# Weight sums in DRAM tied to the heads of the attention, weight pages of half a unit, row sums made later: a two-layer decoder trunk on one core

## The chip, the cores and the metric

The kernel runs on one core of a Trainium2 chip. The metric is device time in microseconds, from the first to the last instruction of one execution, given as the median of the runs shown. Engines are named as in the profile: PE (TensorE matmul), PEld (its weight load), DVE (VectorE), ACT (ScalarE), POOL (GpSimd) and SP (SyncE, which here only issues transfers). SPq and POOLq are the issuing sides of SP and POOL.

## The reference

Two layers, each ending in x <- LayerNorm(alpha * x + sublayer(x)), for 512 positions of width 2048, all in float32. Cut to what matters here:

```python
def even_layer(x, w_in, conv_w, cmp_pos, cmp_w1, cmp_w2, w_out, rel_table):
    h = x @ w_in
    ...
    y_a = a_b * causal_short_conv(a_c * a_h, conv_w) * jax.nn.silu(a_z)
    y_b = nsa_attention(q, k_c, v_c, k_s, v_s, k_w, v_w, gates, rel_table, cmp_pos, cmp_w1, cmp_w2) * jax.nn.silu(b_z)
    return jnp.concatenate([y_a, y_b], axis=-1) @ w_out

def odd_layer(x, w_in, ln_g, ln_b, sgu_w, sgu_b, w_out):
    h = x @ w_in
    uv = jax.nn.gelu(h[..., :2 * D_SGU])
    z = h[..., 2 * D_SGU:]
    u, v = jnp.split(uv, 2, axis=-1)
    v = layer_norm(v, ln_g, ln_b).reshape(bsz, s // SGU_CHUNK, SGU_CHUNK, SGU_GROUPS, SGU_GROUP_DIM)
    w_causal = sgu_w * jnp.tril(jnp.ones((SGU_CHUNK, SGU_CHUNK), sgu_w.dtype))
    mixed = jnp.einsum('gts,bnsgc->bntgc', w_causal, v) + sgu_b.T[:, :, None]
    y = u * mixed.reshape(bsz, s, D_SGU) * jax.nn.silu(z)
    return y @ w_out
```

The attention has 8 query heads. The layer norm of `v` in the odd layer is folded into the position mixing, and for that the kernel needs the sums over `s` of `w_causal`: the row sums of the position weights.

## The kernel before

**Precision.** Each float32 operand is split into a high and a low part (`split`, L84: ACT writes `hi`, DVE writes `lo` = source minus `hi`), and each product is three matmuls, hi x hi, hi x lo and lo x hi.

**Weights.** A *unit* is 1 MB of weights, 128 partitions by 2048 floats. SP loads it in one transfer into a page `raw` (two pages, L90 and L560), ACT and DVE split it in two halves into pages `whi` and `wlo` (four of each), and PE then runs its matmuls. A page is loaded again only after both of its halves have been split.

**Order of the stages**, as PE runs them:

1. The start: `x` (4 MB) and the first two units come in pieces, and 96 matmuls follow (L138 to L157). Then two units of compressed tokens, the rows of the relative bias (`bias_rows`, L174, and `gcol`, L309, which use `raw` pages as scratch; `rrow` and `rscr` go through DRAM by POOL's queue), two key units with `cmp_half` (L273, weights of the compression, also 1 MB in a `raw` page), and the values of group 0.
2. The heads, h = 0 to 7 (L434). Each has six units of 48 matmuls (query, B gate, and four of the convolution), two score branches, softmax and values. `qT` (L445, one buffer) is the scaled query. The bias tiles `bh` (by SP) and `bc` (by POOL, L439 to L443) have two buffers.
3. The first output product, `strassen(sp, wo0, ...)` (L722), then the product for `v`, `strassen(sp, wv1, ...)` (L763). Each is a Strassen-like product of seven half-size products in the order 1, 2, 5, 3, 6, 7, 4, with four units each and 24 matmuls of 512 columns per unit.
4. The units of `u` and `z` (L808, j = 0 to 15, two units each), with the position mixing (L819).
5. The last product, `strassen(sp, wo1, ...)` (L869), and the last layer norm.

**The weight sums.** The products 5, 7, 6 and 4 take sums of weight blocks. They are made in DRAM by POOL's transfer queue (`weight_sums`, L195): for each sum, a copy of one block into a tile `t[q, g, c]` of 1 MB (L204), then a second transfer that adds the other block to it (L206). There are three sets of 16 sums: `sums0` for `wo0`, `sumsv` for `wv1`, `sums1` for `wo1`. A *step* makes two sums by four transfers of 1 MB. The steps of the first two sets are called two to a head (L458), those of `sums1` after every second j (L825). The copies from the weights read only inputs, and nothing but POOL's own queue, and the sums they build on, holds them back.

**Order on the queues.** The instructions of an engine run in the order of its list; that list is made from the program text, from the tiles' buffers and from what each instruction depends on. An instruction that waits holds all that stand behind it on its engine. SP and POOL each take turns through eight semaphores for their transfers, so a transfer also waits for the one eight before it.

**Row sums.** After the `v` product, L788 multiplies a tile of ones with `swT`, the masked position weights, which DVE makes at L778. PE's next unit (`unit_a`, L101) stands behind it.

Of the kernel before, what the change touches and what calls it, by code (L numbers as in the profile page):

```python
# [16 lines left out]
P = 128  # L17
# [48 lines left out]
def trunk(ctx, tc, xT, xn, oneh, cst, table, wa, wv, convw, posT, cw1, cw2, wo0, wuz, wv1, odg, odb, sguw, sgub, wo1, out):  # L66
# [20 lines left out]

    def load_unit(src, n, cut=1024):

        raw = wp.tile([P, 2048], F32, tag="raw", name="raw", bufs=2)  # L90
        nc.sync.dma_start(raw[:, :n], src)
        parts = []
        for c in range(0, n, cut):
            w = min(cut, n - c)
            hi = wp.tile([P, 1024], F32R, tag="hi", name="whi", bufs=4)
            lo = wp.tile([P, 1024], F32R, tag="lo", name="wlo", bufs=4)
            split(hi[:, :w], lo[:, :w], raw[:, c:c + w])
            parts.append((hi, lo))
        return parts
# [35 lines left out]
    for u in range(2):  # L135
        wraw[u] = wp.tile([P, 2048], F32, tag="raw", name="raw", bufs=2)
    xraw = big.tile([P, KT, S], F32, tag="big0", name="xraw")
    for half in range(2):  # L138
        ws = {}
        for u in range(2):  # L140
            ws[u] = (wp.tile([P, 1024], F32R, tag="hi", name="whi", bufs=4), wp.tile([P, 1024], F32R, tag="lo", name="wlo", bufs=4))
        for i, (k0, k1) in enumerate(XCH[half]):
            for u, w0, w1 in WCH[half][i]:
                nc.sync.dma_start(wraw[u][:, half * 1024 + w0:half * 1024 + w1], wa[u][:, half * 1024 + w0:half * 1024 + w1])
            nc.sync.dma_start(xraw[:, k0:k1, :], xT[:, k0:k1, :])
        for i, (k0, k1) in enumerate(XCH[half]):
            for u, w0, w1 in WCH[half][i]:
                split(ws[u][0][:, w0:w1], ws[u][1][:, w0:w1], wraw[u][:, half * 1024 + w0:half * 1024 + w1])
            split(act_hi[:, k0:k1, :], act_lo[:, k0:k1, :], xraw[:, k0:k1, :])
        for k0, k1 in XCH[half]:  # L150
            for u in range(2):
                hi, lo = ws[u]
                for kt in range(k0, k1):
                    w = slice(kt % 8 * P, kt % 8 * P + P)
                    nc.tensor.matmul(first[u], hi[:, w], act_hi[:, kt, :], start=kt == 0, stop=False)
                    nc.tensor.matmul(first[u], hi[:, w], act_lo[:, kt, :], start=False, stop=False)
                    nc.tensor.matmul(first[u], lo[:, w], act_hi[:, kt, :], start=False, stop=kt == KT - 1)  # L157
# [16 lines left out]
    def bias_rows():  # L174
        half = RLEN // 2
        raw = wp.tile([P, 2048], F32, tag="raw", name="raw", bufs=2)
        oh, tb, rr = raw[:RB + 1, 0:RLEN], raw[:RB + 1, RLEN:RLEN + P], raw[:NH, RLEN + P:2 * RLEN + P]
        nc.sync.dma_start(oh, oneh)
        nc.vector.memset(tb, 0.0)
        nc.vector.memset(tb[:, :NH], NEG)  # L180
        nc.sync.dma_start(tb[:RB, :NH], table)
        for c in range(2):
            ps = bank()
            nc.tensor.matmul(ps[:, :half], tb, oh[:, c * half:(c + 1) * half], start=True, stop=True)
            nc.vector.tensor_copy(rr[:, c * half:(c + 1) * half], ps[:NH, :half])
        nc.gpsimd.dma_start(rrow, rr)
        for h in range(NH):
            nc.gpsimd.dma_start(rscr[h], rrow[h:h + 1].to_broadcast([P, RLEN]))
# [6 lines left out]
    def weight_sums(w, name):  # L195
# [3 lines left out]
        def step(q, gcs):  # L199
            def run():  # L200
                for g, c in gcs:
                    t[q, g, c] = dram.tile([P, 2048], F32, name=f"{name}{q}{g}{c}")
                    first = {5: lambda: blk(w, 0, 0, g, c), 7: lambda: blk(w, 1, 1, g, c), 6: lambda: t[7, g, c], 4: lambda: t[6, g, c]}[q]()
                    nc.gpsimd.dma_start(t[q, g, c], first)  # L204
# [11 lines left out]
    with ExitStack() as es:  # L216
# [56 lines left out]
        def cmp_half(kv, c):  # L273
            if c == 0:
                hps[kv] = bank("hp")
            w1 = wp.tile([P, 16, P], F32, tag="raw", name="raw", bufs=2)
            nc.sync.dma_start(w1, cw1[kv, c])
            for l in range(16):
                nc.tensor.matmul(hps[kv][:, :2 * NCMP], w1[:, l, :], toks[kv][:, c, :, c:c + NCMP, l],
# [29 lines left out]
        gcol = wp.tile([P, 2048], F32, tag="raw", name="raw", bufs=2)[:2 * KT, :P]  # L309
# [124 lines left out]
        for h in range(NH):  # L434
# [23 lines left out]
            for st in (steps0 + stepsv)[2 * h:2 * h + 2]:  # L458
                st()
# [60 lines left out]
    def strassen(sp, w, sums, a, done, given=None, more=2, by_tile=False, wx=None):  # L520
# [37 lines left out]
        def unit(p, g, c):  # L558
            src = sums[p, g, c] if p in (5, 7, 6, 4) else blk(w, *{1: (0, 0), 2: (1, 0), 3: (1, 1)}[p], g, c)
            raw = wp.tile([P, 2048], F32, tag="raw", name="raw", bufs=2)  # L560
            nc.sync.dma_start(raw, src)
            parts = []
            for d in range(2):
                pool = wx if wx and count[0] % 2 else wp
# [3 lines left out]
                split(hi, lo, raw[:, d * 1024:(d + 1) * 1024])  # L568
# [204 lines left out]
    with tc.tile_pool(name="sgu", bufs=2) as sg:  # L773
# [12 lines left out]
        for c in range(2):  # L786
            ps = bank()
            nc.tensor.matmul(ps, ones, swT[:, 4 * c:4 * c + 4, :], start=True, stop=True)  # L788
            nc.vector.tensor_copy(rw[:, 4 * c:4 * c + 4, :], ps.rearrange("p (g t) -> p g t", g=4))
# [18 lines left out]
        for j in range(KT):  # L808
# [7 lines left out]
            nc.vector.scalar_tensor_tensor(th, th, 1.0, ps, ALU.add, ALU.mult)  # L816
            pm = bank("pm")
# [7 lines left out]
            if j % 2 and j < 2 * len(steps1):  # L825
                steps1[j // 2]()
# [129 lines left out]
```

## Time and profile before

| what | value |
| --- | --- |
| median of three runs | 1710.26 us (1708.27 to 1713.61) |
| the profiled execution | 1717.5 us; its span 1715.7 us |
| PE busy | 1629.1 us (95%), 7527 matmuls |
| DVE, ACT, POOL busy | 858.7 us, 584.8 us, 124.8 us |
| mean granted clock of PE | 0.978 |
| moved by the DMA engines | 328.50 MB, of it 217.29 MB by SP's queue and 109.60 MB by POOL's |

The span runs from the first to the last instruction, and the profiled execution's own time has 1.8 us around it. "Busy" counts neither the issuing of transfers nor waiting on semaphores. The granted clock is TensorE's share of its full rate, over the stretch named.

### The profile page before, as it was taken

What the parts mean: (1) busy time and instruction counts of PE and PEld (TensorE: products, weight loads), DVE (VectorE), ACT (ScalarE), POOL (GpSimd) and SP (SyncE); (2) the same over time, 40 slices, a digit from 0 to 9 for tenths busy, and PEclk for the clock granted to TensorE, in tenths of its full rate; (3) what the DMA queues carried; (4) which work ended last, traced back from release to release, by engine and by line L of the source; (5) the groups of instructions that cost most, each with busy time, mean ns of one, the idle gap of its engine ahead of it and who ended that gap; (6) DMA issues with size and microseconds to landing.
All of it is one profiled execution on the core that took longest, in us unless ns stands there. A gap on an engine that the chain in (4) does not pass through costs nothing. (4 is left out here: it accounts for less than half of the span.)

```text
span 1715.7 us, 18770 instructions
## 1 busy us (share of the span) xinstructions
PE 1629.1 (95%) x7527; PEld 1349.5 (79%) x7527; DVE 858.7 (50%) x1323; ACT 584.8 (34%) x859; POOL 124.8 (7%) x188
## 2 busy tenths in 40 slices
PE   5789799999999999999999999997999999999995
PEld 3578688888888888888887778885888888888874
DVE  3211444353524444535655977677533333337678
ACT  3111323232323332323454576541222222226531
POOL 1111111111110000000010000000000000000101
PEclk9889899999999999999999999998999999999998
DMA  9999999999998222222476565576422222218763
GB/s 312 271 291 308 283 295 283 282 294 283 281 269 237 80 99 80 78 95 74 165 218 206 197 221 189 179 282 200 134 99 98 91 81 99 98 58 285 234 187 143
DMA packets 70547, 328.50 MB, mean 191 GB/s; under 512 B 7027, under 2 KB 7827, under 8 KB 46652
## 3 DMA queue, kind: packets, MB, share of 16 engines
q1 hardware_dynamic: 39308, 217.29, 35.5%
q0 software_dynamic: 31008, 109.60, 26.4%
q8 instruction: 59, 0.97, 0.2%
q10 hardware_dynamic: 144, 0.41, 0.1%
q14 instruction: 28, 0.23, 0.0%
HBM read 315.72 MB, written 114.84 MB: 251 GB/s over the span
## 5 line engine op out<-in xcount | busy, mean ns | idle before, releaser
L86 DVE TENSOR_TENSOR wlo<-raw,whi 128x1024 fp32r<-128x1024 f32 (+2 forms) x358 | 427.9, 1206 | 653.1 <-ACT whi L85 647.8
L85 ACT CAST whi<-raw 128x1024 fp32r<-128x1024 f32 (+2 forms) x358 | 366.7, 1037 | 970.9 <-PE ps L109 592.9
L108 PE MATMUL ps<-act_hi,whi 128*128 128x512 f32 x1376 | 545.0, 396 | 10.9 <-ACT whi L85 10.9
L110 PE MATMUL ps<-act_hi,wlo 128*128 128x512 f32 x1376 | 539.3, 392 | 0.8 <-DVE wlo L86 0.7
L109 PE MATMUL ps<-act_lo,whi 128*128 128x512 f32 x1376 | 536.9, 390 | 0.0
L108 PEld LDWEIGHTS ps<-act_hi,whi 128*128 128x128 f32 x1376 | 260.1, 189 | 62.6 <-ACT whi L85 11.0
L110 PEld LDWEIGHTS ps<-act_hi,wlo 128*128 128x128 f32 x1376 | 259.3, 188 | 59.1 <-DVE wlo L86 2.3
L109 PEld LDWEIGHTS ps<-act_lo,whi 128*128 128x128 f32 x1376 | 259.7, 189 | 54.0 <-issue 0.3
L585 PE MATMUL ps<-wlo,shi 128*128 128x512 f32 x576 | 228.1, 397 | 9.6 <-DVE wlo L86 9.5
L584 PE MATMUL ps<-whi,shi 128*128 128x512 f32 x576 | 226.0, 396 | 0.6 <-ACT whi L85 0.6
L586 PE MATMUL ps<-whi,slo 128*128 128x512 f32 x576 | 226.5, 394 | 0.0
L585 PEld LDWEIGHTS ps<-wlo,shi 128*128 128x128 f32 x576 | 109.2, 190 | 38.7 <-DVE wlo L86 15.2
L584 PEld LDWEIGHTS ps<-whi,shi 128*128 128x128 f32 x576 | 109.1, 190 | 24.6 <-ACT whi L85 0.9
L586 PEld LDWEIGHTS ps<-whi,slo 128*128 128x128 f32 x576 | 109.2, 190 | 23.6
L206 POOL DMA_DIRECT2D ts<-in_wo_dram x32 | 33.1, 1033 | 277.2 <-DMA ts<-in_wo_dram 142.9
L625 POOL DMA_DIRECT2D xr<-xres x12 | 10.3, 873 | 458.6 <-DMA raw<-ts 409.4
L371 ACT ACTIVATE t_sc<-t_sc,mx 128x128 f32<-128x128 f32 (+1 forms) x64 | 35.1, 550 | 17.0 <-DVE mx L368 17.0
L117 PE MATMUL ps<-whi,act_hi 128*128 128x268 f32 x128 | 36.9, 288 | 2.2 <-ACT whi L85 2.2
L585 PE MATMUL ps<-wlo,act_hi 128*128 128x512 f32 x96 | 38.5, 401 | 0.2 <-DVE wlo L86 0.2
L584 PE MATMUL ps<-whi,act_hi 128*128 128x512 f32 x96 | 38.6, 404 | 0.0
L586 PE MATMUL ps<-whi,act_lo 128*128 128x512 f32 x96 | 38.2, 398 | 0.0
L118 PE MATMUL ps<-wlo,act_hi 128*128 128x268 f32 x128 | 36.9, 288 | 0.6 <-DVE wlo L86 0.6
(201 smaller groups left out, 1366.9 us busy)
## 6 DMA issues: line engine op xcount, KB each, us to landing
raw<-in_wa_dram SPq DMA_DIRECT2D x54, 1024.0 KB, 8.5
ts<-in_wo_dram POOLq DMA_DIRECT2D x32, 1024.0 KB, 13.7
raw<-ts SPq DMA_DIRECT2D x32, 1024.0 KB, 5.1
raw<-in_wuz_dram SPq DMA_DIRECT2D x32, 1024.0 KB, 4.8
raw<-in_wo_dram SPq DMA_DIRECT2D x24, 1024.0 KB, 4.9
tsv<-in_wv_dram POOLq DMA_DIRECT2D x16, 1024.0 KB, 12.5
raw<-tsv SPq DMA_DIRECT2D x16, 1024.0 KB, 4.8
raw<-in_wv_dram SPq DMA_DIRECT2D x12, 1024.0 KB, 4.8
```

The costliest lines, as they stand in the source:

```text
L85: nc.scalar.copy(hi, src)
L86: nc.vector.tensor_tensor(lo, src, hi.bitcast(F32), ALU.subtract)
L108: nc.tensor.matmul(ps, hi[:, w], act_hi[:, kt, :], start=kt == 0, stop=False)
L109: nc.tensor.matmul(ps, hi[:, w], act_lo[:, kt, :], start=False, stop=False)
L110: nc.tensor.matmul(ps, lo[:, w], act_hi[:, kt, :], start=False, stop=kt == KT - 1)
L117: nc.tensor.matmul(ps[:, :width], act_hi[:, kt, ms], hi[:, w], start=kt == 0, stop=False)
L118: nc.tensor.matmul(ps[:, :width], act_hi[:, kt, ms], lo[:, w], start=False, stop=False)
L206: nc.gpsimd.dma_start(t[q, g, c], blk(w, *{5: (0, 1), 7: (0, 1), 6: (0, 0), 4: (1, 0)}[q], g, c), accum_op=ALU.add, max_dma_last_dim=2048)
L371: nc.scalar.activation(t[:, offs[qb]:offs[qb] + nk], t[:, offs[qb]:offs[qb] + nk], AF.Exp, bias=mx[:, qb:qb + 1], accum_out=sm[:, qb:qb + 1])
L584: nc.tensor.matmul(b, s[0][:, k, ms], hi[:, ws], start=new and c == 0 and k == 0, stop=False, **kw)
L585: nc.tensor.matmul(b, s[0][:, k, ms], lo[:, ws], start=False, stop=False, **kw)
L586: nc.tensor.matmul(b, s[1][:, k, ms], hi[:, ws], start=False, stop=c == 1 and k == 3, **kw)
```

## The change

Three edits.

1. **Ties.** A step takes a small piece of an SBUF tile as an argument. Before each copy it sends four bytes of that piece into the sum's tile in DRAM, and the copy that follows overwrites them. The copy must therefore wait for the four bytes to land, and these for the tile that they are read from. In the attention that tile is `qT` of the head; in the units of `u` and `z` it is `ug` of that j. In turn, the next writer of `qT` or of that `ug` buffer has to wait until the four bytes have been read.
2. **Pages.** `raw` becomes four pages of 1024 floats per partition where it was two of 2048. Each unit is loaded by two transfers of 512 KB (rows of 4 KB per partition, where they were 8 KB), and each page is split and freed alone. Scratch uses of `raw` take one or two of the smaller pages.
3. **Row sums.** The two matmuls with `ones` and the two copies of their results move from ahead of the first unit of stage 4 to behind its second.

```diff
+    def raw_page():
+        return wp.tile([P, 1024], F32, tag="raw", name="raw", bufs=4)
+
     def load_unit(src, n, cut=1024):
-        raw = wp.tile([P, 2048], F32, tag="raw", name="raw", bufs=2)
-        nc.sync.dma_start(raw[:, :n], src)
         parts = []
         for c in range(0, n, cut):
             w = min(cut, n - c)
+            raw = raw_page()
+            nc.sync.dma_start(raw[:, :w], src[:, c:c + w])
             hi = wp.tile([P, 1024], F32R, tag="hi", name="whi", bufs=4)
             lo = wp.tile([P, 1024], F32R, tag="lo", name="wlo", bufs=4)
-            split(hi[:, :w], lo[:, :w], raw[:, c:c + w])
+            split(hi[:, :w], lo[:, :w], raw[:, :w])
...
     def bias_rows():
         half = RLEN // 2
-        raw = wp.tile([P, 2048], F32, tag="raw", name="raw", bufs=2)
-        oh, tb, rr = raw[:RB + 1, 0:RLEN], raw[:RB + 1, RLEN:RLEN + P], raw[:NH, RLEN + P:2 * RLEN + P]
+        raw = raw_page()
+        oh, tb, rr = raw[:RB + 1, 0:RLEN], raw[:RB + 1, RLEN:RLEN + P], raw_page()[:NH, :RLEN]
...
         def step(q, gcs):
-            def run():
+            def run(after=None):
+
                 for g, c in gcs:
                     t[q, g, c] = dram.tile([P, 2048], F32, name=f"{name}{q}{g}{c}")
+                    if after is not None:
+                        nc.gpsimd.dma_start(t[q, g, c][0:1, 0:1], after)
...
-            w1 = wp.tile([P, 16, P], F32, tag="raw", name="raw", bufs=2)
-            nc.sync.dma_start(w1, cw1[kv, c])
+            w1 = [raw_page().rearrange("p (l d) -> p l d", d=P) for _ in range(2)]
+            for i in range(2):
+                nc.sync.dma_start(w1[i], cw1[kv, c][:, 8 * i:8 * i + 8])
...
-        gcol = wp.tile([P, 2048], F32, tag="raw", name="raw", bufs=2)[:2 * KT, :P]
+        gcol = raw_page()[:2 * KT, :P]
...
             for st in (steps0 + stepsv)[2 * h:2 * h + 2]:
-                st()
+                st(qT[0:1, 0:1])
...
-            raw = wp.tile([P, 2048], F32, tag="raw", name="raw", bufs=2)
-            nc.sync.dma_start(raw, src)
             parts = []
             for d in range(2):
+                raw = raw_page()
+                nc.sync.dma_start(raw, src[:, d * 1024:(d + 1) * 1024])
...
-                split(hi, lo, raw[:, d * 1024:(d + 1) * 1024])
+                split(hi, lo, raw)
...
-        for c in range(2):
-            ps = bank()
-            nc.tensor.matmul(ps, ones, swT[:, 4 * c:4 * c + 4, :], start=True, stop=True)
-            nc.vector.tensor_copy(rw[:, 4 * c:4 * c + 4, :], ps.rearrange("p (g t) -> p g t", g=4))
+
+        def row_sums():
+            for c in range(2):
+                ps = bank()
+                nc.tensor.matmul(ps, ones, swT[:, 4 * c:4 * c + 4, :], start=True, stop=True)
+                nc.vector.tensor_copy(rw[:, 4 * c:4 * c + 4, :], ps.rearrange("p (g t) -> p g t", g=4))
...
+            if j == 0:
+                row_sums()
             pm = bank("pm")
...
             if j % 2 and j < 2 * len(steps1):
-                steps1[j // 2]()
+                steps1[j // 2](ug[0:1, 0:1])
```

**What moves on POOL at the start.** In the rows below `bc` is a head's bias tile, `ts0_500` the sum of product 5 for `wo0` with g = 0 and c = 0, and the names in brackets are the semaphores waited for (DMASW and DMAHW are transfers of POOL and SP). Before, POOL's list begins like this:

```order
L439 MEMSET bc_848 128x124
L204 DMA ts0_500_1017<-in_wo0_dram 16x16384
L204 DMA ts0_510_1019<-in_wo0_dram 16x16384
L206 DMA ts0_500_1017<-in_wo0_dram 512x512 [waits DMASW0_49]
L206 DMA ts0_510_1019<-in_wo0_dram 512x512 [waits DMASW1_49]
L204 DMA ts0_501_1023<-in_wo0_dram 16x16384
L204 DMA ts0_511_1025<-in_wo0_dram 16x16384
L206 DMA ts0_501_1023<-in_wo0_dram 512x512 [waits DMASW4_49]
L206 DMA ts0_511_1025<-in_wo0_dram 512x512 [waits DMASW5_49]
L439 MEMSET bc_1447 128x124
```

Of the change, the same engine and place, up to the ties of head 0 (`qT_938`), where `rrow` and `rscr` are the bias rows:

```order
L446 MEMSET bc_1488 128x124
L189 DMA rrow_239<-raw_394 8x640 [waits DVE_49]
L191 DMA rscr_240<-rrow_239 128x640 [waits DMASW0_49]
L191 DMA rscr_240<-rrow_239 128x640 x7
L450 COPY bc_871<-bh_869 128x7 [waits DMAHW1_49,Pool_49]
L450 COPY bc_871<-bh_869 128x15
L450 COPY bc_871<-bh_869 128x23
L450 COPY bc_871<-bh_869 128x31
L450 COPY bc_1488<-bh_1486 128x7 [waits DMAHW2_49,Pool_49]
L450 COPY bc_1488<-bh_1486 128x15
L450 COPY bc_1488<-bh_1486 128x23
L450 COPY bc_1488<-bh_1486 128x31
```

```order
L208 DMA ts0_500_1046<-qT_938 1x1 [waits DMASW1_49,Activation_49]
L208 DMA ts0_510_1049<-qT_938 1x1 [waits DMASW2_49]
L208 DMA ts0_501_1054<-qT_938 1x1 [waits DMASW3_49]
L208 DMA ts0_511_1057<-qT_938 1x1 [waits DMASW4_49]
L210 DMA ts0_500_1046<-in_wo0_dram 16x16384 [waits DMASW5_49,DMASW1_49]
L210 DMA ts0_510_1049<-in_wo0_dram 16x16384 [waits DMASW6_49,DMASW2_49]
L212 DMA ts0_500_1046<-in_wo0_dram 512x512 [waits DMASW7_49,DMASW5_49]
L212 DMA ts0_510_1049<-in_wo0_dram 512x512 [waits DMASW6_49,DMASW0_49]
L210 DMA ts0_501_1054<-in_wo0_dram 16x16384 [waits DMASW3_49]
L210 DMA ts0_511_1057<-in_wo0_dram 16x16384 [waits DMASW4_49]
L212 DMA ts0_501_1054<-in_wo0_dram 512x512 [waits DMASW1_49]
L212 DMA ts0_511_1057<-in_wo0_dram 512x512 [waits DMASW2_49]
```

The first sums have moved from the front of POOL's list to behind the bias rows and the `bc` of two heads, and they wait for ACT's write of `qT`. The later heads follow the same pattern: the `bc` of the head after next, then four ties, then eight transfers.

**What moves on PE between stages 3 and 4.** Before, behind the last matmuls of the `v` product (L584 to L586), with `swT` the masked position weights:

```order
L585 MATMUL ps_7931<-wlo_8143,act_hi_5769 128x512
L586 MATMUL ps_7931<-whi_8142,act_lo_5770 128x512
L788 MATMUL ps_8217<-swT_8205,ones_8210 128x512 [waits DVE_49,PE_49]
L788 MATMUL ps_8220<-swT_8205,ones_8210 128x512
L108 MATMUL ps_8233<-act_hi_5769,whi_8225 128x512 [waits Activation_49]
L109 MATMUL ps_8233<-act_lo_5770,whi_8225 128x512
```

Of the change, the end of the second unit of j = 0, 96 matmuls further on:

```order
L112 MATMUL ps_8567<-act_lo_5933,whi_8563 128x512
L113 MATMUL ps_8567<-act_hi_5932,wlo_8564 128x512
L797 MATMUL ps_8619<-swT_8480,ones_8485 128x512 [waits DVE_49,PE_49]
L797 MATMUL ps_8622<-swT_8480,ones_8485 128x512
L830 MATMUL pm_8625<-swT_8480,xv_5920 128x128 x4
L111 MATMUL ps_8647<-act_hi_5932,whi_8637 128x512 [waits Activation_49]
```

The wait for `swT` now stands behind two units of matmuls.

**What moves on POOL at the end of stage 4.** Of the change: the last step, tied to `ug_10742` of j = 15, stands ahead of the residual additions of `wo1` (L632, which are L625 before), where before all sums of `wo1` stood among the heads:

```order
L208 DMA ts1_401_10818<-ug_10742 1x1 [waits DMASW7_49,DVE_49]
L208 DMA ts1_411_10821<-ug_10742 1x1 [waits DMASW0_49]
L210 DMA ts1_401_10818<-ts1_601_10235 16x16384 [waits DMASW7_49]
L210 DMA ts1_411_10821<-ts1_611_10238 16x16384 [waits DMASW0_49]
L212 DMA ts1_401_10818<-in_wo1_dram 512x512 [waits DMASW1_49]
L212 DMA ts1_411_10821<-in_wo1_dram 512x512 [waits DMASW2_49]
L632 DMA xr_8476<-xres_5938 128x512 [waits DMAHW7_49,DMASW5_49,Activation_49]
```

So the 16 sums of `wo1` have moved from the attention into stage 4, and the last two of them reach into the start of stage 5.

## Rows read from the trace of the kernel before

**Rows 1.** The page: the span, and each engine's busy time.

```profile
span 1715.7 us, 18770 instructions
PE 1629.1 (95%) x7527; PEld 1349.5 (79%) x7527; DVE 858.7 (50%) x1323; ACT 584.8 (34%) x859; POOL 124.8 (7%) x188
```

**Rows 2.** Windows of 50 us: length, busy (count) by engine, clock, DMA share, GB/s.

```profile
0.00:50.00 50.00, 31.39 (x98) 21.32 (x98) 16.90 (x23) 17.55 (x20) 8.40 (x17) 0.93 1.00 312
50.00:100.00 50.00, 37.40 (x149) 28.96 (x147) 11.60 (x17) 4.00 (x4) 7.94 (x12) 0.86 1.04 264
100.00:150.00 50.00, 41.71 (x262) 39.11 (x263) 8.83 (x11) 7.85 (x13) 10.19 (x22) 0.90 1.03 305
150.00:200.00 50.00, 40.98 (x228) 36.31 (x227) 16.50 (x41) 12.63 (x27) 6.17 (x8) 0.90 1.03 295
...
300.00:350.00 50.00, 50.00 (x235) 41.99 (x234) 18.97 (x34) 13.90 (x24) 6.17 (x8) 1.00 1.04 281
...
650.00:700.00 50.00, 50.00 (x239) 42.14 (x238) 18.97 (x35) 14.23 (x24) 0.72 (x4) 1.00 0.27 90
...
1600.00:1650.00 50.00, 50.00 (x219) 40.57 (x217) 28.93 (x27) 27.44 (x32) 6.84 (x8) 1.00 0.79 234
```

**Rows 3.** Waits of PE in the first 210 us: total, times, longest.

```profile
PE ps L108 <- ACT whi L85: 10.9, 1, 10.9
PE ps L155 <- ACT act_hi L85: 10.4, 5, 5.6
PE ps L299 <- DVE rep L297: 9.0, 1, 9.0
PE hp L279 <- DMA raw<-in_cw_dram: 6.4, 1, 6.4
```

**Rows 4.** Timeline of POOL at the start: start, duration, [idle before, releaser].

```profile
1.34 1.24 POOL L204 DMA_DIRECT2D ts<-in_wo_dram  x2
...
98.72 4.15 POOL L188 DMA_DIRECT2D rscr<-rrow  x8 [13.91 <-DMA rrow<-raw]
```

**Rows 5.** Timeline of PE at the start: the first matmul, and two at the slow rate.

```profile
5.55 0.80 PE L155 MATMUL ps<-act_hi,whi 128*128 128x512 f32 x1 [5.55 <-ACT act_hi L85]
...
12.32 0.63 PE L157 MATMUL ps<-act_hi,wlo 128*128 128x512 f32 x1
12.74 0.63 PE L155 MATMUL ps<-act_hi,whi 128*128 128x512 f32 x1
```

**Rows 6.** Windows of 5 us around the row sums, columns as in rows 2.

```profile
1165.00:1170.00 5.00, 0.29 (x1) 0.32 (x2) 4.12 (x7) 0.00 (x0) 1.37 (x1) 0.50 0.80 280
1170.00:1175.00 5.00, 5.00 (x13) 2.86 (x13) 3.17 (x7) 0.00 (x0) 0.00 (x0) 0.73 0.50 170
```

**Rows 7.** All waits of PE: those for the position weights and in the Strassen products.

```profile
PE ps L788 <- DVE swT L778: 10.0, 1, 10.0
PE ps L585 <- DVE wlo L86: 9.7, 9, 3.2
```

**Rows 8.** Timeline of POOL in the attention: the sums of one pair of tiles.

```profile
213.43 1.39 POOL L204 DMA_DIRECT2D tsv<-in_wv_dram  x2
230.93 1.04 POOL L206 DMA_DIRECT2D tsv<-in_wv_dram  x1 [16.11 <-DMA tsv<-in_wv_dram]
...
234.04 0.89 POOL L204 DMA_DIRECT2D tsv<-in_wv_dram  x1
```

**Rows 9.** Timeline of ACT: the `qT` of heads 1 and 2.

```profile
263.03 0.59 ACT L446 ACTIVATE qT<-ps 128x512 f32<-128x512 f32 x1
338.87 0.59 ACT L446 ACTIVATE qT<-ps 128x512 f32<-128x512 f32 x1
```

**Rows 10.** DMA issues: count, KB each, median us from issue to landing.

```profile
raw<-in_wuz_dram SPq DMA_DIRECT2D x32, 1024.0 KB, 4.8
xres<-xr SPq DMA_DIRECT2D x12, 256.0 KB, 2.2
raw<-in_table_dram SPq DMA_DIRECT2D x1, 1.0 KB, 8.4
```

More of the change, by code (lines that the diff above doesn't have):

```diff
@@ L135, in trunk @@
     for u in range(2):
-        wraw[u] = wp.tile([P, 2048], F32, tag="raw", name="raw", bufs=2)
+        wraw[u] = [raw_page(), raw_page()]
     xraw = big.tile([P, KT, S], F32, tag="big0", name="xraw")
@@ L143, in trunk @@
             for u, w0, w1 in WCH[half][i]:
-                nc.sync.dma_start(wraw[u][:, half * 1024 + w0:half * 1024 + w1], wa[u][:, half * 1024 + w0:half * 1024 + w1])
+                nc.sync.dma_start(wraw[u][half][:, w0:w1], wa[u][:, half * 1024 + w0:half * 1024 + w1])
             nc.sync.dma_start(xraw[:, k0:k1, :], xT[:, k0:k1, :])
@@ L147, in trunk @@
             for u, w0, w1 in WCH[half][i]:
-                split(ws[u][0][:, w0:w1], ws[u][1][:, w0:w1], wraw[u][:, half * 1024 + w0:half * 1024 + w1])
+                split(ws[u][0][:, w0:w1], ws[u][1][:, w0:w1], wraw[u][half][:, w0:w1])
             split(act_hi[:, k0:k1, :], act_lo[:, k0:k1, :], xraw[:, k0:k1, :])
@@ L275, in cmp_half @@
                 hps[kv] = bank("hp")
-            w1 = wp.tile([P, 16, P], F32, tag="raw", name="raw", bufs=2)
-            nc.sync.dma_start(w1, cw1[kv, c])
+            w1 = [raw_page().rearrange("p (l d) -> p l d", d=P) for _ in range(2)]
+            for i in range(2):
+                nc.sync.dma_start(w1[i], cw1[kv, c][:, 8 * i:8 * i + 8])
             for l in range(16):
-                nc.tensor.matmul(hps[kv][:, :2 * NCMP], w1[:, l, :], toks[kv][:, c, :, c:c + NCMP, l],
+                nc.tensor.matmul(hps[kv][:, :2 * NCMP], w1[l // 8][:, l % 8, :], toks[kv][:, c, :, c:c + NCMP, l],
                                  start=c == 0 and l == 0, stop=c == 1 and l == 15)
```

## The prediction

> **What bounds the kernel now.** I read the page first: PE is busy for 1629.1 of 1715.7 us, so 86.6 us of idle time and the time that PE works below its full clock are all that this change can give back [rows 1]. Then the windows, to see where they lie. From 200 us on nearly every window is full at clock 1.00, as the one at 300 us; the first four have 31.4, 37.4, 41.7 and 41.0 us busy of 50, at clocks of 0.93, 0.86, 0.90 and 0.90 [rows 2]. So 48.5 us of the idle time lie in the first 200 us. The DMA engines are full there (share 1.00 to 1.04), and the waits of PE name what is missing: weight splits, pieces of `x`, a page of `cw`, and a DVE instruction that stands behind a split [rows 3]. POOL sends its first copies at 1.34 us, before anything needs a sum [rows 4]. At 300 us the DMA engines are as full and PE loses nothing [rows 2]: there a unit takes PE 48 matmuls, while the start needs 6 MB before PE can run freely. So the sums hurt only at the start.
>
> Of the rest, one wait of 10.0 us belongs to the row sums and nine of 9.7 us together to late `wlo` in Strassen products [rows 7]. The tail is left alone.
>
> **The ties, at the start.** First the work: busy time weighted with the clock is 31.4 x 0.93 + 37.4 x 0.86 + 41.7 x 0.90 + 41.0 x 0.90 = 135.8 us at full clock, done in 200 us [rows 2]. 64 us are lost, 48.5 to idling and 15.7 to the clock.
>
> With the sums gone from the front, what remains? The first matmul cannot come much before 5.55 us [rows 5]. The first block needs 6.3 million bytes (`x` and two units). At a DMA share of 0.27 the engines moved 90 GB/s, so full engines move about 333 GB/s [rows 2]; 6.3 MB then take 19 us, after some 3 us of first landing, and the last piece still needs split and matmuls, about 5 us. The block ends near 30 us as far as data goes. PE needs 96 matmuls at 0.228 us (219 in a full window of 50 us [rows 2]), 21.9 us; those at the start run at half clock, 0.42 us apart [rows 5]. I take 33 us for the end of the block, 11 us above its work. Behind it each unit takes PE 10.9 us (48 x 0.228), and a load of 1 MB 4.8 us [rows 10]: loads are ahead. Three places can still cost a little: the scratch pages of the bias rows, which SP must wait for; `rrow` and `rscr`, on which the `bh` loads in SP's queue wait, with weights queued behind them (POOL needed 13.9 us to get `rrow` landed and `rscr` begun, behind a copy [rows 4]; now nothing stands ahead); and the compression pages. I give these 4 us. The front then takes 135.8 + 11 + 4 = 151 us: **gain 49 us**. Upper bound: only the first 5.55 us are lost, gain 59. Lower bound: two of the long waits stay for another reason (10.9 us for a page that the bias rows hold, 9.0 us behind DVE's order [rows 3]) with some of the clock: gain 28.
>
> **The ties, in the heads.** 48 of these four-byte transfers are issued by POOL, at about 0.9 us each by a POOL transfer in the rows [rows 8]: POOL is at 7% [rows 1], so the issue itself is covered. What matters is whether a head's eight transfers fit in a head. Two heads' `qT` lie 75.8 us apart [rows 9]. One pair of tiles, from copies to next copies, takes 234.04 - 213.43 = 20.6 us under full engines [rows 8]; two pairs 41 us, and the last additions some 17 us more, by the 17.5 us from copies to additions. The landing of four bytes is in no row; it lies between 2.2 us (256 KB on quiet engines) and 8.4 us (1 KB on full ones) [rows 10]; I take 5 us, since the engines are half loaded. So a head's sums end 63 us after its `qT`, and POOL's list is free after 46 us. The next `qT`, which must wait for the ties of this head, comes at 75.8 us: no wait. Behind POOL's waits stand the `bc` tiles of the head after next, needed a whole head later. The full DMA engines now reach to the end of the attention, and the window at 300 us shows what that costs PE: nothing. Product 5 of `wo0` needs sums of head 0, and `wv1` sums of heads 4 to 7, long done. Cost 0; without that slack, it is the rival below.
>
> **The ties, in stages 4 and 5.** A step comes every four units, 43.6 us, and takes 5 + 18 + 17 = 40 us even on full engines, which they aren't there. The last step, tied to j = 15, falls on the first 40 us of `wo1`. There PE needs 1 MB in 24 x 0.228 = 5.5 us, 190 GB/s; the window at 1600 us shows 234 GB/s at a share of 0.79, so 296 GB/s on full engines [rows 2]. Loads and 4.2 MB of sums over 40 us want 190 + 105 = 295: just full. If both queues got half, loads would lack 42 GB/s, 1.7 MB in 40 us, worth 9 us of PE; pages loaded and split ahead hold about three units, 16 us. I take **2 us of loss**, bounds 0 and 10.
>
> **Pages.** The splits stay as they are (1024 wide); SP issues about 180 more transfers. On the gain side, a half can be split when it lands, and its page is free without the other half: of the 9.7 us for `wlo` [rows 7] I take 4, bounds 0 and 10. On the loss side, a load of 512 KB is in no row: it lies between 2.2 us for 256 KB and 4.8 us for 1 MB [rows 10], 3.1 us if straight between them. Two that overlap then cost what one did. Since four pages can be in flight, I take no loss; one after the other they cost 6.2 us per unit, which is a rival.
>
> The Trainium skill (page "DMA: Bandwidth & Descriptors", section "Measured (HBM→SBUF, 128 partitions, SWDGE, issued from GpSimd)") has a rule against this edit: batch transfers to at least 1 MiB. By the fit in its section "Anatomy of one DMA", 2.0 us and bytes over 436 GB/s, I estimate 4.4 us for a unit and 3.2 us for a half. The 4.8 us of 1 MB [rows 10] are 0.4 us above the fit; no row has a half.
>
> **Row sums.** PE stood still for 10.0 us until `swT` was made [rows 7], and then ran at a clock of 0.73 for the window behind [rows 6], 1.3 us lost of 5. Now 96 matmuls, 21.8 us, stand between, and the weights of the first unit were split before the wait began. **Gain 11 us**, bounds 8 and 12. The two row sums themselves stay; `rw` is read after them, by DVE, at `mb`.
>
> **Sum.** -49 - 11 - 4 + 2 = -62 us on the span of 1715.7 us: 1653.7. The profiled execution took 1717.5 us, 7.2 above the median of 1710.26; I take the same difference off the median: **1648 us**.
>
> **The rivals.**
>
> *Other side: the heads wait for the sums.* If a head's POOL work outlasts a head, the next `qT` waits for ties that POOL has not issued, and the attention runs at the pace of the sums. It decides at 75.8 us against my 46, that is, when a pair takes 35 us instead of 20.6 [rows 8, 9]. At 45 us a pair, POOL is free after 95, each of seven heads loses 19 us, and the time is 1648 + 133 = 1781 us. Against it: 20.6 us was measured under full engines.
>
> *Other side: halves cost as much as wholes in a row.* If the two halves of a unit do not overlap, the 84 units of the Strassen products come every 6.2 us while PE takes 5.5: 84 x 0.7 = 59 us, and 4 us of gain gone: 1711 us; a little more by the row of 4.8 us. Against it: 333 GB/s over all engines is 1 MB in 3.2 us, which only overlapping loads reach.
>
> By the page's fit two halves in a row take 6.4 us, and I estimate 84 x 0.9 = 76 us and 1728 us in all.
>
> *The front is only half freed.* If the long waits come from page order and not from shared engines, the front gives about 25 us, near its lower bound: 1672 us. For it: the 10.9 us wait stands at a page that the bias rows held [rows 3]; against it: that page was held by `rrow`, which stood behind sums on POOL [rows 4].
>
> *The start of `wo1` stalls.* The 9 us above, without the cover: 1655 us, within the range.
>
> That the change does nothing can be left out: in the new order the copies stand behind the ties.
>
> **Chances.** Forecast (1630 to 1664 us) 0.70; front half freed (1664 to 1690) 0.17; halves in a row 0.06; heads paced by the sums 0.05; nothing within noise 0.02. 0.3% of the time, 5 us, is about what can be told from no change. The range of 8 in 10 reaches from 1630, where front and pages give their upper bounds, to 1674, which takes in most of the half-freed case. Faster: 0.70 + 0.17 and a third of the halves case, 0.89; same 0.03; slower 0.08.
>
> **What would show it.** In the changed profile the first 150 us should have PE busy for all but about 15 us, POOL's first copy should come behind the first `qT`, near 110 us, and the DMA share should be well under 1 before it. A wait of `qT` on a tie, or of PE on `ps_s` in the heads, shows the first rival; more waits of PE for `wlo` between the attention and stage 4 the second. No wait of PE for `swT` should be left; if DVE is late there with `wlo` instead, the gain of 11 us shrinks. I am wrong if PE still idles over 30 us before head 0.

## The result, and the profile after

| | before | after |
| --- | --- | --- |
| median of four runs each | 1710.2 us (1708.27 to 1713.61) | **1639.2 us** (1635.04 to 1641.72) |
| ratio | | 0.958 (0.9552 to 0.9609) |
| the profiled execution; its span | 1717.5 us; 1715.7 us | 1635.04 us; 1633.0 us |

The change makes the kernel 71 us faster; 62 us were forecast. The page after, beside [rows 1]:

```profile
span 1633.0 us, 19377 instructions
PE 1603.1 (98%) x7527; PEld 1335.9 (82%) x7527; DVE 859.1 (53%) x1323; ACT 589.6 (36%) x859; POOL 150.7 (9%) x236
```

The same matmuls now take 26 us less of busy time, and PE idles for 29.9 us of the span where it idled for 86.6. The windows beside [rows 2] (length, busy (count) by engine, clock, DMA share, GB/s):

```profile
0.00:50.00 50.00, 42.92 (x171) 34.39 (x172) 23.97 (x32) 20.64 (x23) 1.01 (x7) 0.97 0.54 186
50.00:100.00 50.00, 48.72 (x292) 42.78 (x291) 13.72 (x18) 9.31 (x14) 6.30 (x17) 1.00 0.63 219
100.00:150.00 50.00, 49.33 (x299) 44.30 (x298) 19.02 (x50) 16.26 (x34) 6.23 (x10) 1.00 0.65 196
150.00:200.00 50.00, 50.00 (x241) 42.09 (x241) 22.36 (x44) 14.36 (x29) 2.95 (x7) 1.00 0.71 193
...
650.00:700.00 50.00, 50.00 (x241) 42.09 (x240) 22.81 (x45) 15.13 (x30) 2.06 (x2) 1.00 0.79 205
...
1450.00:1500.00 50.00, 45.71 (x201) 36.27 (x199) 28.34 (x26) 20.72 (x24) 4.16 (x6) 1.00 0.86 271
```

PE loses 9.0 us in its first 150, and the engines are no longer full there. They are busier in the heads (0.79 at 650 us, where it was 0.27), at no cost to PE. A new gap stands at the start of `wo1`. The waits of PE over the whole execution, beside [rows 3, 7] (total, times, longest):

```profile
PE ps L158 <- ACT act_hi L85: 6.8, 2, 4.8
PE ps L591 <- ACT ua L643: 4.3, 2, 2.5
PE ps L113 <- DVE wlo L86: 1.3, 1, 1.3
PE ps L306 <- DVE rep L304: 0.7, 1, 0.7
```

No wait for `swT` is left, and only 0.2 us for `wlo` in the Strassen products. POOL's timeline beside [rows 4, 8] (start, duration, [idle before, releaser]):

```profile
57.37 0.74 POOL L189 DMA_DIRECT2D rrow<-raw  x1 [55.81 <-DVE lnT L320]
62.21 4.23 POOL L191 DMA_DIRECT2D rscr<-rrow  x8 [4.10 <-DMA rrow<-raw]
...
127.51 2.08 POOL L208 DMA_DIRECT2D ts<-qT  x4 [48.15 <-ACT qT L453]
131.56 1.04 POOL L210 DMA_DIRECT2D ts<-in_wo_dram  x2 [1.96 <-DMA ts<-qT]
...
163.77 1.02 POOL L212 DMA_DIRECT2D ts<-in_wo_dram  x1 [2.07 <-DMA ts<-in_wo_dram]
```

The bias rows are sent at 57 us with nothing ahead of them, and POOL waits 4.1 us for `rrow` to land where it waited 13.9 [rows 4]. The first sums follow the first `qT`, which comes at 126.6 us (the prediction had said near 110). A head's four ties and eight transfers are issued in 36 us. `qT` of the heads beside [rows 9]:

```profile
126.62 0.59 ACT L453 ACTIVATE qT<-ps 128x512 f32<-128x512 f32 x1
...
207.37 0.59 ACT L453 ACTIVATE qT<-ps 128x512 f32<-128x512 f32 x1
```

The later heads stand 75.8 us apart as before, but for one gap that is 121.7 us in both kernels. The DMA issues beside [rows 10] (count, KB each, median us from issue to landing):

```profile
raw<-in_wuz_dram SPq DMA_DIRECT2D x64, 512.0 KB, 4.9
ts<-qT POOLq DMA_DIRECT2D x16, 0.0 KB, 3.5
ts<-ug POOLq DMA_DIRECT2D x16, 0.0 KB, 2.3
```

Where the time came from, read from start times in the traces (us), with the experiments told of below: "front" is `qT` of head 1, `wo0` runs from its first matmul to that of the next product, `wv1` from its first matmul to its third-last, "pm" is the first position mixing, and `wo1` runs from the last mixing to the start of the last matmul. `qT` of head 0 would be a poor mark: PE's list has 664 matmuls ahead of it before the change, 640 after and 711 in e1, but 1031 ahead of that of head 1 in every kernel of the table.

| kernel | median | front | wo0 | wv1 | pm | wo1 |
| --- | --- | --- | --- | --- | --- | --- |
| before | 1710.2 | 263.0 | 168.2 | 162.9 | 1195.0 | 161.5 |
| after | 1639.2 | 207.4 | 156.5 | 158.6 | 1111.6 | 162.2 |
| e1, no ties | 1683.4 | 262.6 | 156.6 | 158.7 | 1167.0 | 155.9 |
| e2, whole pages | 1679.7 | 224.5 | 167.9 | 161.1 | 1142.6 | 175.7 |
| e3, rows early | 1647.5 | 207.8 | 156.3 | 158.7 | 1123.0 | 164.1 |
| e4, last set untied | 1681.7 | 262.6 | 156.4 | 158.6 | 1166.7 | 155.9 |
| e5, three a head | 1631.5 | 207.1 | 158.7 | 158.7 | 1113.6 | 156.6 |
| e6, four a head | 1647.9 | 207.5 | 156.8 | 158.7 | 1131.1 | 155.9 |
| e8, e5 with whole pages | 1666.8 | 222.8 | 169.0 | 160.3 | 1141.2 | 161.4 |
| e9, tied to rrow | 1655.0 | 227.2 | 156.4 | 158.7 | 1131.4 | 162.7 |
| e10, halves in whole pages | 1652.5 | 212.1 | 157.6 | 159.2 | 1118.1 | 169.4 |

Before to after, the front gives 55.7 us, `wo0` 11.7 and `wv1` 4.3; `pm` is 83.4 us earlier, of which the row sums are the remaining 11.7; `wo1` loses 0.7. The sum is 82.7, the difference of the two spans; the medians differ by 71, since the profiled execution of before lies 7.3 us above its median and that of after 4.2 below.

### The profile page after: what moved, and what is told of

Its sections match the earlier page's. It is cut to its first block, busy times and chain, and to the rows that moved or that the text cites. A ratio compares the mean times of both kernels' runs of the same rounds, so it can differ in the third digit from the quotient of the medians.

```text
span 1633.0 us, 19377 instructions
## 1 busy us (share of the span) xinstructions
PE 1603.1 (98%) x7527; PEld 1335.9 (82%) x7527; DVE 859.1 (53%) x1323; ACT 589.6 (36%) x859; POOL 150.7 (9%) x236
## 4 chain that ended last, share of the span: by engine, by line
PE 93%; issue 2%; DVE 2%; DMA 2%; ACT 0%; POOL 0%; SPq 0%; POOLq 0%; DVEq 0%
PE ps L111 19%; PE ps L113 19%; PE ps L112 19%; PE ps L593 8%; PE ps L592 8%; PE ps L591 8%; PE ps_t L397 1%; PE ps L122 1%; PE ps L120 1%; PE ps L121 1%; PE hp L286 1%; PE pm L830 1%; PE po L340 1%; PE po L342 1%; PE po L341 1%
## 5 line engine op out<-in xcount | busy, mean ns | idle before, releaser
L85 ACT CAST whi<-raw 128x1024 fp32r<-128x1024 f32 (+2 forms) x358 | 371.1, 1038 | 908.8 <-PE ps L112 568.7
L212 POOL DMA_DIRECT2D ts<-in_wo_dram x32 | 33.2, 1038 | 161.5 <-DMA ts<-in_wo_dram 82.5
L677 POOL TENSOR_TENSOR rs<-mv,epst 128x1 f32<-128x1 f32 x12 | 14.7, 1232 | 287.9 <-DVE mv L675 287.9
L122 PE MATMUL ps<-whi,act_lo 128*128 128x268 f32 x128 | 36.9, 288 | 0.0
```

The costliest lines, as they stand in the source:

```text
L85: nc.scalar.copy(hi, src)
L122: nc.tensor.matmul(ps[:, :width], act_lo[:, kt, ms], hi[:, w], start=False, stop=kt == KT - 1)
L212: nc.gpsimd.dma_start(t[q, g, c], blk(w, *{5: (0, 1), 7: (0, 1), 6: (0, 0), 4: (1, 0)}[q], g, c), accum_op=ALU.add, max_dma_last_dim=2048)
```

## The experiments

Diffs are against the changed kernel unless said otherwise. Each has four runs or more, and its ratio is to the kernel before on the same chip.

**e1: without the ties.**

```diff
-                st(qT[0:1, 0:1])
+                st()
...
-                steps1[j // 2](ug[0:1, 0:1])
+                steps1[j // 2]()
```

> The change without its ties: half pages and late row sums stay, the sums in DRAM start at the front again. Theory (the sums take the DMA engines' time while PE still waits for its first weights): the front loses what the ties gave, about 50 us, and the start of the last product gets back some 5 us; about 1685 us, first qT near 170 us. Rival (the small pages alone unclog the front, because a scratch page no longer holds a whole unit): 1660 us or less, first qT before 150 us.

Measured: 1683.42 us, ratio 0.9823 (0.9799 to 0.9848). The first window of 50 us:

```profile
0.00:50.00 50.00, 33.19 (x103) 22.96 (x104) 18.58 (x25) 17.64 (x20) 8.40 (x17) 0.90 1.00 302
```

and the largest wait of PE in all:

```profile
PE ps L111 <- ACT whi L85: 13.9, 2, 10.1
```

The front is that of before to half a microsecond (262.6 against 263.0), with the engines at share 1.00: the smaller pages give nothing while the sums run there. The ties are worth 44 us in the change: 55.2 at the front, less the 6.3 that `wo1` gains when no step reaches into it, by trace. The first `qT` came at 187.6 us, not near 170; 71 more matmuls stand ahead of it than in the changed kernel.

**e2: ties and late row sums, with pages of a whole unit** (`load_unit`, `unit`, `cmp_half` and the scratch pages as before the change).

```diff
...
+            raw = wp.tile([P, 2048], F32, tag="raw", name="raw", bufs=2)
+            nc.sync.dma_start(raw, src)
             for d in range(2):
-                raw = raw_page()
-                nc.sync.dma_start(raw, src[:, d * 1024:(d + 1) * 1024])
```

> The change without its pages: ties and late row sums on pages of a whole unit. Theory (the 12 us that the first output product and the 4 us that the v product got shorter come from pages that are freed in halves): about 1655 us, and the first output product takes 168 us again as before the change. Rival (they come from the ties, since no sums crowd the end of the attention): within 4 us of 1639 us.

Measured: 1679.68 us, ratio 0.9799 (0.9768 to 0.983). So the pages are worth about 40 us in the change, far above every expectation; only `wo0` took the 168 us that were expected. By the table 17.1 lie at the front, 11.4 in `wo0`, 2.5 in `wv1` and 13.5 in `wo1`. At the front SP waits for a page that the scratch `gcol` holds until PE has transposed it. SP's waits between 40 and 110 us, of e2 and of the changed kernel:

```profile
SPq L91 <- PE ps L314: 16.8, 1, 16.8
```

```profile
SPq L97 <- PE ps L319: 16.7, 1, 16.7
```

The wait is the same. But in the changed kernel a fourth page is free, and SP issues half a unit ahead of it, at 39.08 us:

```profile
39.08 17.51 SPq L97 DMA_DIRECT2D raw<-in_wa_dram  x2
```

In e2 the next unit is issued behind the wait, at 57.7 us, and PE waits for weights, where the changed kernel shows no such wait. All waits of PE, of e2 and of e10 (below), which also keeps the scratch on whole pages:

```profile
PE ps L108 <- ACT whi L85: 8.9, 2, 6.2
```

```profile
PE ps L110 <- ACT whi L85: 5.3, 1, 5.3
```

In `wo0` the same work stands in the windows from its first to its last matmul, here of the kernel before:

```profile
828.00:996.00 168.00, 161.99 (x705) 130.54 (x704) 120.10 (x143) 90.21 (x110) 12.31 (x14) 0.98 0.64 207
```

and of the kernel after:

```profile
772.00:928.50 156.50, 156.50 (x707) 129.26 (x707) 121.25 (x145) 93.61 (x112) 12.32 (x14) 1.00 0.73 225
```

Only 6.0 of the 11.5 us were idle time of PE. The other 5.5 were longer busy time. A clock of 0.98 makes about 3 of them; that the rest are matmuls behind a late split is likely, not shown. ACT's waits in the same two stretches say why. Before:

```profile
ACT whi L85 <- DMA raw<-ts: 23.3, 8, 5.3
ACT whi L85 <- PE ps L586: 18.5, 8, 6.9
ACT whi L85 <- DMA raw<-in_wo_dram: 12.4, 5, 3.6
```

After:

```profile
ACT whi L85 <- PE ps L593: 42.6, 29, 3.1
...
ACT whi L85 <- DMA raw<-ts: 2.0, 3, 1.2
```

Before, the split waited 35.7 us for weights to land; now it waits 2.0 us for weights, and otherwise for PE to give back a split page, so the loads are ahead.

**e3: row sums where they were** (the loop of two matmuls and two copies back ahead of stage 4).

> The change with the row sums made early again. Theory: PE waits about 10 us for the masked position weights and the clock costs 1 to 2 more, about 1651 us. Rival (DVE's late splits would have held PE there anyway, so the row sums only covered another wait): 1645 us or less.

Measured: 1647.46 us, ratio 0.9615 (0.9588 to 0.9642). PE waits again for `swT`:

```profile
PE ps L795 <- DVE swT L785: 8.3, 1, 8.3
```

`pm` is 11.4 us later than after, by trace, 11.0 of it between `wv1` and `pm`; the medians differ by 8 us. The time lies between the two expected, but the wait is the theory's: DVE's late splits did not stand in for it.

**e5: all sums in the heads, three steps to a head, none in stage 4.**

```diff
-            for st in (steps0 + stepsv)[2 * h:2 * h + 2]:
+            for st in (steps0 + stepsv + steps1)[3 * h:3 * h + 3]:
...
-            if j % 2 and j < 2 * len(steps1):
-                steps1[j // 2](ug[0:1, 0:1])
```

> The change with all 24 steps tied to the heads, three to a head, and none in the stage of u and z. Theory (the start of the last product lost about 5 us to the last step's transfers; three steps take POOL 5 + 3 x 21 = 68 us of a head's 76, so no query waits): about 1634 us, no wait of PE for ua at the start of the last product. Rival (the heads wait for their ties when the sums fill a head): over 1660 us, with qT more than 80 us apart.

Measured: 1631.54 us, ratio 0.9522 (0.9497 to 0.9547). The heads are as far apart as in the changed kernel, and `wo1` takes 156.6 us where that needs 162.2: the last step, tied to j = 15, costs 5.6 us there. The first 40 us of `wo1` show how. With the last step beside them (the changed kernel), and without it (e5), the loads land in:

```profile
raw<-in_wo_dram SPq DMA_DIRECT2D x10, 512.0 KB, 11.0
```

```profile
raw<-in_wo_dram SPq DMA_DIRECT2D x10, 512.0 KB, 5.5
```

In the changed kernel ACT stands still for such a load, and its copies of PE's results into `ua`, for which PE waits 4.3 us, stand behind the split:

```profile
1479.62 1.05 ACT L85 CAST whi<-raw 128x1024 fp32r<-128x1024 f32 x1 [8.83 <-DMA raw<-in_wo_dram]
```

Run once more beside the changed kernel on one chip:

> The changed kernel as it is, beside three steps a head on the same chip: 1635 to 1643 us.

> Three steps a head, as in e5, beside the changed kernel on the same chip. If the 7 us between them are real, 1630 to 1634 us against 1636 to 1642 us; if they came from the chip, the two agree within 5 us.

The changed kernel took 1635.57 us (1632.92 to 1638.8), ratio 0.9549 (0.9524 to 0.9575); three a head 1629.85 us (1629.23 to 1631.18), ratio 0.9518 (0.9494 to 0.9542). All six runs of the one lie below all five of the other: three a head is 5.7 us (0.3%) faster than the changed kernel.

**e6: four steps to a head** (as e5, with 4 for 3).

> All 24 steps are tied, four to a head in heads 0 to 5, none in the units of u and z. It tests the point from which the rival of waiting heads decides. Theory of the prediction (a pair of tiles takes 20.6 us, two pairs 41): four steps keep POOL for 5 + 82 = 87 us of a head of 75.8 us, so each of the heads 1 to 6 comes about 11 us late, qT of heads 0 to 6 stands about 87 us apart, and the time is about 1632 + 66 = 1698 us. Rival: with the weight loads of the heads alone beside it a step takes the 18 us seen in the changed kernel (36 us from its ties to its last additions), four take 72 us, the heads stay 73 to 76 us apart, and the time is that of three steps a head, 1628 to 1636 us.

Measured: 1647.86 us, ratio 0.9617 (0.9594 to 0.9641): between the two. `qT` now waits for its own ties, by the waits of all engines:

```profile
ACT qT L453 <- DMA ts<-qT: 25.3, 2, 21.8
...
PE ps_s L359 <- ACT qT L453: 14.7, 2, 12.5
ACT qT L453 <- DMA tsv<-qT: 11.6, 1, 11.6
```

Three of the seven gaps between heads grow, two shrink, and the seven take 600.5 us where they took 581.6: 19 us in all, not 11 for each head. The rival's mechanism exists, then, and begins between three and four steps a head. The four bytes land late:

```profile
ts<-qT POOLq DMA_DIRECT2D x32, 0.0 KB, 13.4
```

Full engines alone do not do that. With three steps a head (e5), ties that are issued on full engines, but with no other transfer of POOL's under way, land soon. A window around five of them, and their landing:

```profile
632.90:637.00 4.10, 4.10 (x20) 3.39 (x19) 1.09 (x2) 0.86 (x2) 3.09 (x6) 1.00 1.00 322
```

```profile
ts<-qT POOLq DMA_DIRECT2D x5, 0.0 KB, 3.0
```

What the late ones share is POOL's own earlier transfers. The last tie of head 0 in e5 is issued at 166.2 us with three of POOL's 1 MB transfers still under way. Its window, and its landing, 0.3 us after the last of the three:

```profile
166.20:184.00 17.80, 17.80 (x91) 15.18 (x90) 10.43 (x25) 6.86 (x15) 1.17 (x4) 1.00 0.95 253
```

```profile
ts<-qT POOLq DMA_DIRECT2D x1, 0.0 KB, 17.5
```

In e6 the first tie of head 1, with two ahead, takes 12.1 us and lands 0.2 us after the second.

**e4: the last 16 sums alone without ties.**

```diff
-                steps1[j // 2](ug[0:1, 0:1])
+                steps1[j // 2]()
```

> The sums of wo1 (16 of 48) lose their ties and stand at the front of POOL's list again; the other 32 keep theirs. If what counts is whether the engines are full while the first units come, a third of the sums is as bad as all of them, since eight pairs at 20.6 us cover the first 165 us: qT of head 0 near 185 us, and 1675 to 1690 us. If the loss goes with the bytes: a third of the 44 us, about 1650 us. If only the late page of the bias rows mattered (rrow behind sums on POOL): some 14 to 20 us of loss, 1653 to 1660 us.

Measured: 1681.74 us, ratio 0.9819 (0.9795 to 0.9843): a third of the sums is as bad as all of them (e1). At the front its windows are:

```profile
0.00:50.00 50.00, 32.95 (x91) 22.06 (x92) 16.60 (x21) 16.39 (x19) 8.41 (x17) 0.93 1.00 299
...
150.00:200.00 50.00, 39.67 (x212) 34.40 (x212) 15.14 (x33) 12.35 (x24) 7.18 (x10) 0.90 1.02 292
200.00:250.00 50.00, 50.00 (x239) 41.95 (x238) 23.00 (x60) 17.46 (x39) 7.05 (x13) 1.00 1.02 260
```

So the loss does not go with the bytes: it is there when the sums run during the first 200 us, and sums that run on behind them cost nothing. But in both kernels the bias rows also stand behind the sums on POOL: `rrow` is sent at 89.2 us in e1 and at 86.4 in e4, and at 57.4 after the change. Full engines and late rows are not separated by these two.

**e9: head ties that read `rrow`.** The expectation speaks of all ties; the kernel as run changes those of the heads alone (32 sums), and the sums of `wo1` keep `ug`.

```diff
-                st(qT[0:1, 0:1])
+                st(rrow[0:1, 0:1])
```

> All ties read rrow (a DRAM tile that is written at about 57 us) where they read qT and ug, so the sums of all three sets run from some 62 us on, as fast as POOL's queue takes them. Theory of the prediction (full engines hurt only while x and the first units come): PE is as busy from 62 us on as in the changed kernel, qT of head 0 stands at 127 to 132 us, and the time is 1633 to 1645 us. Rival: full engines cost PE until the attention's steady units, as the windows of 100 to 200 us of the kernel before suggest (8 to 9 us lost in each): qT of head 0 near 145 us or later, and 1650 to 1665 us.

Measured: 1654.99 us, ratio 0.9662 (0.9642 to 0.9682). The rival's number, not the theory's. The bias rows are on time here (`rrow` at 57.8 us). The windows:

```profile
100.00:150.00 50.00, 45.70 (x256) 40.15 (x255) 10.84 (x16) 10.94 (x21) 6.64 (x10) 0.90 0.98 278
150.00:200.00 50.00, 42.22 (x195) 35.46 (x194) 24.43 (x70) 15.63 (x36) 8.21 (x12) 0.93 1.00 282
300.00:350.00 50.00, 50.00 (x238) 42.17 (x238) 24.68 (x65) 17.60 (x37) 10.55 (x16) 1.00 0.98 263
```

and the page loads that were issued between 62 and 200 us:

```profile
raw<-in_wa_dram SPq DMA_DIRECT2D x19, 512.0 KB, 8.7
```

In the changed kernel the same pages land in 4.0 us between 50 and 127 us. So full engines cost PE 19.8 us of the front even when `x` and the first units are in, and nothing at 300 us. Why the stretch to 200 us is hurt and the later ones are not is not shown. Of the 55.2 us that e1 loses at the front, 15.5 lie in the first block of 96 matmuls (the next matmul starts at 48.5 us in e1, at 33.0 after the change), before `rrow` is sent in any kernel; with the 19.8 of e9 some 20 us are left, which no run divides between full engines and late bias rows.

**e8: three a head with whole pages** (e2 with the edit of e5).

> Pages of a whole unit (as in e2) with the ties three to a head (as in e5), so that no sum is made in stage 4 or at the start of wo1. If the 13.6 us that whole pages lost in wo1 in e2 came from meeting the last step's sums, wo1 takes about 156 us here and the time is 1664 to 1668 us. If whole pages slow each Strassen product by themselves, as the 11 us in wo0 suggest, wo1 still takes 166 us or more and the time is 1674 to 1680 us. By either, qT of head 0 comes near 139 us and wo0 takes about 168 us.

Measured: 1666.81 us, ratio 0.973 (0.9708 to 0.9752). The time is that of the first theory, but `wo1` takes 161.4 us, between the two: without sums beside it whole pages cost 4.8 us there (161.4 against 156.6), with the last step 13.5 (175.7 against 162.2). The other 8.7 us of e2 in `wo1` come with the last step's sums beside whole pages.

**e10: two transfers of a half into one whole page** (against e2; shown for `unit`, and the same in `load_unit` and `cmp_half`).

```diff
-            nc.sync.dma_start(raw, src)
+            for d in range(2):
+                nc.sync.dma_start(raw[:, d * 1024:(d + 1) * 1024], src[:, d * 1024:(d + 1) * 1024])
```

> As e2 (two pages of a whole unit, ties and late row sums as in the changed kernel), but each unit and each page of cw comes by two transfers of 512 KB into the one page. So the first half can be split when it has landed, while the page is still loaded again only after both halves are split. If the smaller pages gain by being freed one by one, this runs like e2: qT of head 0 near 139 us, wo0 in 166 to 169 us, 1675 to 1682 us. If they gain by the earlier landing of the first half, it runs like the changed kernel: wo0 in 156 to 159 us, 1638 to 1650 us. Between the two: both count, in the share that it shows.

Measured: 1652.49 us, ratio 0.9647 (0.9619 to 0.9675): some 27 of the 40 us of the pages, and 16.9 us above the changed kernel run on the same chip. SP issues the two halves of a unit within 0.4 us of each other. For the units of `tsv`, by issue and landing times, the first half lands 3.9 us after its issue and the pair is in after 5.1, where a whole unit of e2 takes 4.8. `wo0` takes 157.6 us, nearly as after, so there the earlier first half is what counts. At the front e10 gets back 12.4 of the 17.1 us; the other 4.7 are near the 5.3 us for which PE still waits behind the scratch page. `wo1` (7.2 above after) also needs pages that come free one by one.

## Why the prediction was right, and where its terms were off

**The mechanism at the front held.** The copies stand behind the first `qT`, the engines are at 0.54 to 0.65 there, and e1 and e4 show that untied sums bring the loss back. 49 us were forecast and 55.7 came. The first block ended as forecast (33 us): the next work starts, before and after, at

```profile
49.72 0.39 PE L108 MATMUL ps<-act_hi,whi 128*128 128x512 f32 x1
```

```profile
33.02 0.39 PE L111 MATMUL ps<-act_hi,whi 128*128 128x512 f32 x1
```

The 4 us of small stalls are 2.0 (1.3 and 0.7 in PE's waits). What was off is the work. The sum counts 31.4 x 0.93 = 29.2 us of work at full clock in the first window of before, but its 98 matmuls are 22.3 us at 0.228 each. So it left 9.8 us for the block to gain (20.8 lost, 11 kept), and the block gained 16.7; those 6.9 are about the 6.7 by which the front beat the forecast.

Two sentences of the argument fell. "The sums hurt only at the start" is true of the first 200 us, not of the cold start that the sum worked with: e9, with a free cold start and sums from some 62 us on, still loses 19.8 us by the front. And the gain is not the ties' alone: with whole pages (e2) the front gains 38.5 us, and the pages, worth 0.4 there without ties (e1), give the other 17.1. The term of 49 us was worked out for the ties; that it came so near is in part luck.

**Pages were the mis-sized term.** 4 us, with bounds 0 and 10, stand in the sum; in the products the traces show 11.7 + 4.3 = 16.0, and the change without them is 40 us slower. The price was read from PE's idle time before `wlo` alone [rows 7], which is about half of what a late split cost, and not from ACT's waits for landing. Nor did the sum look at the front, or at what whole pages do beside the last step. The loss side, "no loss", held: a half lands in 4.9 us where a whole took 4.8 [rows 10], above the 3.1 us estimated, but halves overlap (5.1 us for a pair in e10), and behind the first block PE waits only 2.1 us in all for split weights.

The rule of the Trainium skill that the prediction weighed (page "DMA: Bandwidth & Descriptors", section "Measured (HBM→SBUF, 128 partitions, SWDGE, issued from GpSimd)": batch to at least 1 MiB, measured there on transfers that GpSimd issues) does not decide here: e10 changes nothing against e2 but the size of the transfers, which SP issues, and is 27 us faster. The price of smaller transfers shows in the engines' time. SP's queue of e2 (packets, MB, share of 16 engines' span):

```profile
q1 hardware_dynamic: 39308, 217.29, 36.2%
```

and of e10:

```profile
q1 hardware_dynamic: 65228, 217.30, 38.7%
```

36.2% of 1677.9 us is 607 us, 38.7% of 1647.5 is 638: the same bytes take 5% more.

**Row sums**: 11 forecast, 11.7 by trace, 8 by the medians of e3. Right, and no wait of PE for DVE took the place of this one.

**The heads**: cost 0, right. POOL's work for a head was put at 46 us and took 36; four bytes landed in 3.5 us where 5 was estimated. The rival that heads wait was placed at POOL work of 75.8 us; e6 shows it, at four steps a head.

**The start of `wo1`**: 2 us of loss forecast, 5.6 measured (after against e5), inside its bounds. The mechanism was the forecast one, loads that land late beside the last step, but the units held ahead covered less than the 16 us assumed. The trace before and after shows only 0.7, because the pages give 4.8 there (e8 against e5).

**The other rivals**: the half-freed front (1672 us) and halves in a row (1711) are out, by 1639.2 us and by the waits above. By the spans the sum of 62 us fell 20.7 short of 82.7: 12.0 by the pages, 6.7 by the front, 0.7 by the row sums and 1.3 in `wo1`. The medians show only 9 of it. The prediction took the profiled execution to lie above the median by as much after the change as before; it lay 7.3 above, then 4.2 below, and that this made up for 11.5 us of the shortfall is luck.

## What to carry to other kernels

Background transfers between DRAM tiles are best held back until the loads of the start are through, and a four-byte transfer from a tile that the path makes is enough to hold them. Spread them so that each share has landed before the next tie is issued: here the path began to wait for its own ties between three and four steps a head. Size the gain of smaller pages by what the split waits for (landing, or a page given back), not by PE's idle time alone. Look at the scratch tiles that borrow load pages: a free page beside them let a load go ahead of the wait here, worth some 5 us by e10's wait, which no run isolates.

## What the hardware did that was not expected

Four bytes are not always quick. With no other transfer of POOL's under way they landed in 1.5 to 4.5 us (the changed kernel and e5), also with the engines at a share of 1.00. Issued while POOL's own 1 MB transfers were under way, they took 12.1 us (e6) and 17.5 us (e5) and landed 0.2 and 0.3 us after the last of these: in this trace a tie comes in behind what POOL's queue still holds.

A single half of a megabyte took as long to land as a whole one (4.9 and 4.8 us), but two that were issued together were in after 5.1 us (`tsv`, e10).
